# A hybrid decoder layer on one core: the second group's input norm placed beside the first group's attention

## The chip, the cores and the metric

One core of a Trainium2 chip runs the whole layer as one program. The metric is the device time of one execution in microseconds (us), lower being better. Five engines work side by side, each through its own instructions in a fixed order: PE (matrix products and transposes), DVE (elementwise work, reductions, the search for the largest values), ACT (functions and copies), POOL (here it issues the gathers of expert rows) and SP (it issues the other DMA transfers).

## What is computed

1024 tokens of width 1024 pass through one layer: a norm, a projection, retention in 4 heads beside differential attention in 4 heads, an output projection, and then a mixture of 16384 one-neuron experts of which each token uses 128 (8 heads with 16 each).

```
h = rmsnorm(x, norm_mix_g)
rq, rk, rv, rg, dq, dk, dv = split(h @ w_in)
ret_out  = silu(rg) * rmsnorm(retention(rq, rk, rv))
diff_out = rmsnorm(diff_attention(dq, dk, dv, lam), diff_subln_g) * (1 - li)
x = x + concat(ret_out, diff_out) @ w_out
xn = rmsnorm(x, norm_ffn_g)
s = einsum(xn @ peer_wq, subkeys)        # 2 x 128 scores per token and head
pick the 16 largest of each half, then the 16 largest sums: e, g = softmax
x = x + sum over the chosen e of g * gelu(u[e] . xn) * v[e]
out = rmsnorm(x, final_norm_g)
```

## The kernel before

**Groups.** The tokens are cut in tiles of 128. The first group, called sparse, holds tiles 0 to 2, the second, called dense, tiles 3 to 7 (`GROUPS`, line 39). Both pass through the generator `front` (line 140), whose steps are: norm of the input and its transposition (`normed`, line 241, inside `split_t`, line 210); the projections `rv` and `dv` (lines 261 and 262); per head the projections of queries and keys, retention and attention (lines 275 to 404); the gate projection `rg` (line 408); the output projection (lines 423 to 427); a second norm and transposition; and the routing (lines 452 to 492), which in 16 passes projects a query (`psT`, line 458), copies it out of PSUM (`pqT`, line 459), takes scores against 128 keys (`psc`, `sc`, lines 467 and 469) and finds the 16 largest on DVE (lines 473 to 477, and after every second pass 479 to 491). After it the experts of the sparse group are gathered row by row by POOL (lines 891 and 898) and used by DVE, while PE computes all 16384 experts for the dense group (lines 740 to 742 and 818 to 820).

**Numbers in two halves.** A projection writes each operand as a rounded part and a rest and makes three products of it, so every weight chunk of 512 KB is loaded (`wraw`), rounded by ACT (`whi`, line 164) and, in the sparse group, subtracted by DVE (`wlo`, line 166) and stored for the dense group, which loads it again (line 163). Each product of `mm` (line 170) is three matmuls, lines 172 to 174.

**Order.** The generators yield at their seams. `weave(a, b, na, nb)` takes `na` steps of one for `nb` of the other, and `until(g, mark)` runs one to a named seam. Lines 766 to 773 set the order that this change is about:

```
run(until(gs, "mixed"))                                            # sparse attention to its end
run(weave(until(gs, "summed"), until(gd, "normed"), 15, 5))        # output projection | dense input norm
run(weave(until(gd, "projected"), gs, 8, 19))                      # dense rv, dv | sparse routing
```

This is only the order of the program. A planner (`schedule_with_timeline_sim`, line 62) then places the instructions on each engine, in the program's order where nothing speaks against it and otherwise where it expects room, so that later matmuls can stand ahead of earlier ones that have to wait.

**Memory.** PSUM has eight banks: tag `A` twice two banks, `B` twice one, `T` one and `R` one. The sparse group's query projections all use `T` (`proj_t`, line 179). `proj_n` (line 189) takes two tiles at a time in `A`, and the fifth tile of the dense group in `R`. The dense group's input tiles `xt`, its norm weights `gmix` and the scratch `jk` share five rooms of tag `ug` (`big`, line 152). `Routed` (line 494) takes the rooms `sx`, `sa` (sparse) and `la`, `lb` (dense) when it is made.

Of the kernel before, what the change touches and what calls it, by code (L numbers as in the profile page):

```python
# [23 lines left out]
P = 128  # L24
# [75 lines left out]
def layer_kernel(ctx, tc, x, wt, wn, wo, wq, sk, ut, u, v, gmix, gffn, gfin, gsub, dlam, consts, alb, out):  # L100
# [39 lines left out]
    def front(m, pp, cst, g0, nt, dense, late):  # L140
# [11 lines left out]
        def big(shape, name, dt=F32):  # L152
            return m.big[0].tile(shape, dt, tag=m.big[1], bufs=m.big[2], name=name)
# [32 lines left out]
                res.append((a, b, ps))  # L186
            return res

        def proj_n(srcs, xs, done):
            ps = []  # L190
            while len(ps) < nt:
                if nt - len(ps) == 1 and dense:
                    ps.append(pp.tile([P, 512], F32, tag="R", name="psN1"))
                else:
                    two = bankA("psN2")
                    ps += [two[:, 0], two[:, 1]]
            for c, src in enumerate(srcs):
                w = chunk(src, [P, 2, 512])
                for t in range(nt):
                    for k in range(2):  # L200
                        dc = 2 * c + k
                        mm(ps[t], at(xs, slice(None), dc, slice(t * P, (t + 1) * P)), at(w, slice(None), k),
                           dc == 0, dc == DC - 1)
                if c < len(srcs) - 1:
                    yield
            for t in range(nt):
                done(t, ps[t])
            yield
# [17 lines left out]


        def x_in(t):
            xt = big([P, D], "xt")
            SY.dma_start(xt, x[g0 + t])  # L230
            return xt
        if first:
            xts = [x_in(0)]
            gm = m.fp.tile([P, D], F32, tag="R", name="gmix")
        else:
            gm = big([P, D], "gmix")
        SY.dma_start(gm, gmix.to_broadcast([P, D]))
        if first:
            xts += [x_in(t) for t in range(1, nt)]
# [1 line left out]
        def normed(t):  # L241
            ms = m.tp.tile([P, 1], F32, tag="ms", bufs=2, name="ms")
            xt = xts[t] if first else x_in(t)
            jk = m.fp.tile([P, D], BF, tag="yd", name="jk") if first else big([P, D], "jk", BF)
            A.activation(jk, xt, AF.Square, accum_out=ms)
            r = rstd(m.tp, ms, D, "x")
            V.scalar_tensor_tensor(xt, xt, r, gm, op0=ALU.mult, op1=ALU.mult)
            return xt
# [9 lines left out]
            A.activation(dvt, ps, AF.Copy)  # L258
            SY.dma_start(dv_d[g0 + t], dvt)

        yield from proj_n([WN + c for c in range(4)], hx, lambda t, ps: A.activation(rv[:, t], ps, AF.Copy))
        yield from proj_n([WN + 8 + c for c in range(4)], hx, put_dv)
        yield "projected"

        fp, ap = m.fp, m.ap
# [184 lines left out]
        late.nx = nx  # L450

        yield "routing"
        tv = fp.tile([P, nt, PH, 2, K], F32, tag="yd", name="tv")
        ti = fp.tile([P, nt, PH, 2, K], U32, tag="R", name="ti")
        for hp in range(2 * PH):
            h = hp // 2
            qT = wp.tile([P, n], F32, tag="ga", bufs=2, name="pqT")
            for a, b, ps in proj_t(WQ + hp, nx, "TR"):
                A.activation(qT[:, a:b], ps, AF.Copy)
            skt = fp.tile([P, NK], F32, tag="at", bufs=2, name="skt")  # L460
            SY.dma_start(skt, sk[hp])
            sc = fp.tile([P, nt, NK], F32, tag="kT", bufs=2, name="sc")
            for t0 in range(0, nt, 4):
                t1 = min(nt, t0 + 4)
                ps = bankB("psc")
                for t in range(t0, t1):
                    PE.matmul(ps[:, (t - t0) * P:(t - t0 + 1) * P], qT[:, t * P:(t + 1) * P], skt,
                              start=True, stop=True)
                A.activation(sc[:, t0:t1], ps[:, :(t1 - t0) * P].rearrange("p (t k) -> p t k", k=NK), AF.Copy)
            for t in range(nt):  # L470
                a, b = tv[:, t, h, hp % 2], ti[:, t, h, hp % 2]
                s = sc[:, t]
                V.max(a[:, :8], s)
                V.max_index(b[:, :8], a[:, :8], s)
                V.match_replace(s, a[:, :8], s, LOW)
                V.max(a[:, 8:], s)
                V.max_index(b[:, 8:], a[:, 8:], s)
            if hp % 2:
                V.tensor_copy(late.tf[:, :nt, h], ti[:, :, h])
                cd = fp.tile([P, nt, NC2], F32, tag="q20", bufs=2, name="cd")  # L480
                for o, i0, ni, nj in ((0, 0, 2, 16), (32, 2, 2, 8), (48, 4, 4, 4), (64, 8, 8, 2)):
                    V.tensor_tensor(cd[:, :, o:o + ni * nj].rearrange("p t (i j) -> p t i j", j=nj),
                                    tv[:, :, h, 0, i0:i0 + ni, None].to_broadcast([P, nt, ni, nj]),
                                    tv[:, :, h, 1, None, :nj].to_broadcast([P, nt, ni, nj]), op=ALU.add)
                for t in range(nt):
                    c, a, b = cd[:, t], late.cv[:, t, h], late.ci[:, t, h]
                    V.max(a[:, :8], c)
                    V.max_index(b[:, :8], a[:, :8], c)
                    V.match_replace(c, a[:, :8], c, LOW)
                    V.max(a[:, 8:], c)  # L490
                    V.max_index(b[:, 8:], a[:, 8:], c)
            yield

    class Routed:


        def __init__(self, rp, nt, tags):
            n = nt * PH * K
            both = rp.tile([P, 2, n], F32, tag=tags[0], name="late0")
            self.tf = both[:, 0].bitcast(F16).rearrange("p (t h s k) -> p t h s k", t=nt, h=PH, s=2)  # L500
            self.cv = both[:, 1].rearrange("p (t h k) -> p t h k", t=nt, h=PH)
            self.ci = rp.tile([P, nt, PH, K], U32, tag=tags[1], name="late1")
# [183 lines left out]

    gates = []

    def last_dve():
        ins = nc.cur_bb.bb.instructions  # L690
        return next(i for i in reversed(ins) if i.engine == V.engine).name
# [11 lines left out]
    def run(g):  # L703
        for _ in g:
            pass
# [48 lines left out]
    with ExitStack() as es:  # L754
        pf = pool("pf", es, space=bass.MemoryType.PSUM)
        ms, md = SimpleNamespace(), SimpleNamespace()
        with ExitStack() as e2:
# [8 lines left out]
            with ExitStack() as e3:  # L766
                ms.ap = pool("fa", e3)
                run(until(gs, "normed"))
                run(islice(gs, 4))
                front_consts(cst, cp, ms.ap)  # L770
                run(until(gs, "mixed"))
            run(weave(until(gs, "summed"), until(gd, "normed"), 15, 5))
            run(weave(until(gd, "projected"), gs, 8, 19))
        with ExitStack() as e2:
            fd = pool("fd", e2)
            md.tp = md.ap = md.fp = fd
# [92 lines left out]

    def gate(ins):  # L870
        nonlocal nth
        tc.add_manual_dep(ins.ins, gates[min(nth, len(gates) - 1)],
                          mybir.DependencyInfo(mybir.DependencyClass.NoSync, mybir.DependencyReason.DATA),
                          reason="pace of the gathered experts")
        nth += 1

    def row(t, i, name):
# [62 lines left out]
```

## Time and profile before

| | |
|---|---|
| median of 3 runs | 2811.94 us (2809.43 to 2814.86) |
| the profiled execution | 2812.24 us |
| its span | 2810.5 us |
| PE busy | 2681.3 us, 95% |
| DVE busy | 2303.7 us, 82% |
| ACT busy | 997.4 us, 35% |
| POOL busy | 1071.4 us, 38% |

The span is cut by the events of the order above. The sparse group's projections and attention run to about 160 us, its gate projection from 159 to 181, the output projection and the dense input norm to 266, the sparse routing beside the dense `rv` and `dv` to 400, the dense attention to some 800, the dense routing to 980, and the experts from there to the end. Busy shares are averages over all of these, so each question is read from the stretch that it is about.

### The profile page before, as it was taken

The numbers are of one execution on the slowest core, as the hardware profiler recorded it, in microseconds if no ns is written. First come the engines' busy times: TensorE is split into PE (matmuls) and PEld (weight loads), VectorE is DVE, ScalarE is ACT, GpSimd is POOL, SyncE is SP. The second block draws the span as 40 slices with busy tenths as digits, with TensorE's granted clock in tenths as the row PEclk, the third lists the DMA queues.
The fourth block names the chain that finished last, engine by engine and source line by source line (L and its number), as shares of the span: only waits on it lengthen the run. The fifth ranks groups of instructions, "written<-read, shape, count | busy, mean of one in ns | idle before, by whom it ended". The sixth has DMA issues, their size and how long they took to land.

```text
span 2810.5 us, 43147 instructions
## 1 busy us (share of the span) xinstructions
PE 2681.3 (95%) x16043; PEld 2421.6 (86%) x16043; DVE 2303.7 (82%) x4496; ACT 997.4 (35%) x1879; POOL 1071.4 (38%) x782
## 2 busy tenths in 40 slices
PE   7979989888889999999999999999999999999998
PEld 6867888776789999998888888999999999899997
DVE  3554789887478989986999998888998889889987
ACT  4553335554233356772222222222222222223222
POOL 0000004543310000003555556665666567765662
PEclk9989999999989999999999999999999999999999
DMA  7546557877853347799999899898999989989995
GB/s 265 188 177 231 194 191 254 292 276 259 305 193 132 112 150 244 240 281 330 347 347 338 337 374 354 325 348 336 327 344 338 341 333 346 352 317 341 337 348 204
DMA packets 302076, 797.46 MB, mean 284 GB/s; under 512 B 25116, under 2 KB 119336, under 8 KB 297768
## 3 DMA queue, kind: packets, MB, share of 16 engines
q1 hardware_dynamic: 190120, 390.41, 39.2%
q0 software_dynamic: 111744, 404.28, 39.0%
q8 instruction: 126, 2.06, 0.3%
q14 instruction: 86, 0.70, 0.1%
HBM read 698.97 MB, written 95.62 MB: 283 GB/s over the span
## 4 chain that ended last, share of the span: by engine, by line
PE 66%; DVE 8%; DMA 5%; issue 4%; POOL 2%; ACT 1%; SPq 0%; POOLq 0%; DVEq 0%; ACTq 0%
PE psH L742 7%; PE psH L741 7%; PE psH L740 7%; PE psV L818 5%; PE psV L819 5%; PE psV L820 5%; PE kp L820 3%; PE kp L819 3%; PE kp L818 3%; PE psHs L740 3%; PE psHs L742 3%; PE psHs L741 3%; PE psG L613 3%; DVE ug L893 2%; DMA ug<-in_u,idx 2%
## 5 line engine op out<-in xcount | busy, mean ns | idle before, releaser
L891 POOL DMA_INDIRECT ug<-in_u,idx x384 | 529.9, 1380 | 903.5 <-ACT st L615 458.0
L898 POOL DMA_INDIRECT vg<-in_v,idx x384 | 536.1, 1396 | 393.8 <-DVE sa L900 289.8
L893 DVE SCALAR_TENSOR_TENSOR ug<-ug,sx 128x1024 f32<-128x1024 f32 x384 | 458.7, 1223 | 55.5 <-DMA ug<-in_u,idx 54.7
L900 DVE SCALAR_TENSOR_TENSOR sa<-vg,shs,sa 128x1024 f32<-128x1024 f32 x384 | 492.0, 1281 | 10.5 <-DMA vg<-in_v,idx 6.2
L741 PE MATMUL psH<-nl,uh 128*128 128x320 f32 x1424 | 439.5, 309 | 0.0
L740 PE MATMUL psH<-nh,uh 128*128 128x320 f32 x1424 | 439.3, 309 | 0.0
L742 PE MATMUL psH<-nh,ul 128*128 128x320 f32 x1424 | 438.3, 309 | 0.3 <-DVE ul L728 0.3
L818 PE MATMUL psV<-vh,wh 128*128 128x512 f32 x768 | 300.0, 392 | 1.1 <-DVE accl L854 1.1
L819 PE MATMUL psV<-vl,wh 128*128 128x512 f32 x768 | 299.8, 391 | 0.0
L740 PEld LDWEIGHTS psH<-nh,uh 128*128 128x128 f32 x1424 | 267.3, 188 | 5.8
L741 PEld LDWEIGHTS psH<-nl,uh 128*128 128x128 f32 x1424 | 267.3, 188 | 4.8
L742 PEld LDWEIGHTS psH<-nh,ul 128*128 128x128 f32 x1424 | 267.0, 188 | 4.3 <-DVE ul L728 0.6
L726 ACT ACTIVATE uh<-uraw 128x1024 fp32r<-128x1024 f32 x128 | 135.8, 1061 | 321.5 <-PE psH L741 218.0
L743 ACT ACTIVATE ga<-psH 128x320 f32<-128x320 f32 x178 | 75.1, 429 | 447.0 <-PE psH L742 434.2
L740 PE MATMUL psHs<-nh,uh 128*128 128x320 f32 x624 | 195.7, 315 | 6.8 <-ACT ga L743 6.8
L819 PE MATMUL kp<-vl,wh 128*128 128x512 f32 x512 | 200.1, 393 | 0.3 <-DVE vl L842 0.3
L818 PE MATMUL kp<-vh,wh 128*128 128x512 f32 x512 | 194.7, 393 | 4.7 <-ACT wh L834 4.7
L164 ACT ACTIVATE whi<-wraw 128x1024 fp32r<-128x1024 f32 x104 | 109.9, 1058 | 241.2 <-PE psT L173 124.8
L741 PE MATMUL psHs<-nl,uh 128*128 128x320 f32 x624 | 194.1, 311 | 0.0
L742 PE MATMUL psHs<-nh,ul 128*128 128x320 f32 x624 | 192.6, 313 | 0.8 <-DVE ul L728 0.8
L728 DVE TENSOR_TENSOR ul<-uraw,uh 128x1024 fp32r<-128x1024 f32 x128 | 156.9, 1226 | 44.1 <-ACT uh L726 43.9
L820 PE MATMUL psV<-vh,wl 128*128 128x512 f32 x456 | 173.3, 389 | 0.0
(251 smaller groups left out, 6036.4 us busy)
## 6 DMA issues: line engine op xcount, KB each, us to landing
uraw<-in_ut SPq DMA_DIRECT2D x128, 512.0 KB, 6.6
vraw<-in_v SPq DMA_DIRECT2D x128, 512.0 KB, 6.9
g_d<-st SPq DMA_DIRECT2D x80, 512.0 KB, 6.3
gt<-g_d SPq DMA_DIRECT2D x32, 1280.0 KB, 9.6
wl_d<-wlo SPq DMA_DIRECT2D x52, 512.0 KB, 2.9
wlo<-wl_d SPq DMA_DIRECT2D x52, 512.0 KB, 4.3
wraw<-in_wt SPq DMA_DIRECT2D x32, 512.0 KB, 4.4
wraw<-in_wq SPq DMA_DIRECT2D x32, 512.0 KB, 4.6
```

The costliest lines, as they stand in the source:

```text
L726: A.activation(uh, raw, AF.Copy)
L728: V.tensor_sub(ul, raw, uh.bitcast(F32))
L740: PE.matmul(ps, uh[:, dc], xh[:, dc, sl], start=(dc == 0), stop=False)
L741: PE.matmul(ps, uh[:, dc], xl[:, dc, sl], start=False, stop=False)
L742: PE.matmul(ps, ul[:, dc], xh[:, dc, sl], start=False, stop=(dc == DC - 1))
L818: PE.matmul(ps, Wh[e][:, sl], Vh[e][:, so], start=start, stop=False)
L819: PE.matmul(ps, Wh[e][:, sl], Vl[e][:, so], start=False, stop=False)
L820: PE.matmul(ps, Wl[e][:, sl], Vh[e][:, so], start=False, stop=stop)
L891: G.indirect_dma_start(out=ug, out_offset=None, in_=u, in_offset=bass.IndirectOffsetOnAxis(ap=idxA[t][:, k:k + 1], axis=0))
L893: gate(V.scalar_tensor_tensor(ug, ug, 1.0, xt, op0=ALU.mult, op1=ALU.mult, accum_out=hs[:, k:k + 1]))
L898: G.indirect_dma_start(out=vg, out_offset=None, in_=v, in_offset=bass.IndirectOffsetOnAxis(ap=idxA[t][:, k:k + 1], axis=0))
L900: gate(V.scalar_tensor_tensor(ac, vg, hs[:, k:k + 1], ac, op0=ALU.mult, op1=ALU.add))
```

## The change

1. **Order.** The sparse group first goes to its seam "projected" and six steps on; then its attention is woven with the dense input norm, six steps to one. Seven steps of the sparse group follow (four of the gate projection, three of the transposition of its results), then four steps of the dense group (its `rv` projection), then the rest of the output projection. Only `dv` is left to be woven with the sparse routing.
2. **Pace and rooms.** The five dense input tiles use the rooms `sx`, `sa` and `rv` in turn, `gmix` the room `la`, `jk` the room `lb`. Each load of a tile is tied, in the planner's order alone, behind the last DVE instruction that the program held when the load was written. `Routed` takes its rooms when the routing begins.
3. **Banks.** The dense `rv` takes bank `T` and `dv` a bank `B` for the fifth tile in place of `R`. The sparse routing's passes use banks `T` and `R` in turn.

```diff
-        def proj_n(srcs, xs, done):
+        def proj_n(srcs, xs, done, odd="R"):
...
-                    ps.append(pp.tile([P, 512], F32, tag="R", name="psN1"))
+                    ps.append(bankB("psN1") if odd == "B" else pp.tile([P, 512], F32, tag=odd, name="psN1"))
...
         def x_in(t):
-            xt = big([P, D], "xt")
-            SY.dma_start(xt, x[g0 + t])
+            rooms = ((sp, "sx"), (sp, "sa"), (lp, "rv"))[t % 3]
+            xt = rooms[0].tile([P, D], F32, tag=rooms[1], name="xt") if dense else big([P, D], "xt")
+            ins = SY.dma_start(xt, x[g0 + t])
+            if dense:
+                after(ins, last_dve(), "input of the second group")
...
-            gm = big([P, D], "gmix")
+            gm = lp.tile([P, D], F32, tag="la", name="gmix")
...
-            jk = m.fp.tile([P, D], BF, tag="yd", name="jk") if first else big([P, D], "jk", BF)
+            jk = m.fp.tile([P, D], BF, tag="yd", name="jk") if first else lp.tile([P, D], BF, tag="lb", name="jk")
...
-        yield from proj_n([WN + c for c in range(4)], hx, lambda t, ps: A.activation(rv[:, t], ps, AF.Copy))
-        yield from proj_n([WN + 8 + c for c in range(4)], hx, put_dv)
+        yield from proj_n([WN + c for c in range(4)], hx, lambda t, ps: A.activation(rv[:, t], ps, AF.Copy), "T")
+        yield from proj_n([WN + 8 + c for c in range(4)], hx, put_dv, "B")
...
         yield "routing"
+        late.alloc()
...
-            for a, b, ps in proj_t(WQ + hp, nx, "TR"):
+            for a, b, ps in proj_t(WQ + hp, nx, "TR" if dense else "TR"[hp % 2]):
...
-                run(until(gs, "mixed"))
-            run(weave(until(gs, "summed"), until(gd, "normed"), 15, 5))
-            run(weave(until(gd, "projected"), gs, 8, 19))
+                run(until(gs, "projected"))
+                run(islice(gs, 6))
+                run(weave(until(gs, "mixed"), until(gd, "normed"), 6, 1))
+            run(islice(gs, 4 + sn))
+            run(islice(gd, 4))
+            run(until(gs, "summed"))
+            run(weave(until(gd, "projected"), gs, 4, 19))
```

The number of instructions of each kind stays as it was on every engine, but for eight more `ACT_TABLE_LOAD` on ACT. Rows of the built programs show what moved. In them `xt` is a dense input tile, `rg` and `yd` are the sparse group's results of retention and attention, `psX` is a bank of transposes, `ret` and `psS`, `psA`, `pov` are retention's and attention's banks, `hh`/`hl` are the transposed inputs (here the dense group's) and `mh` the transposed results.

**Place 1, PE, between the sparse gate projection and the output projection.** Before, retention's last tile, then:

```order
L293 MATMUL ret<-qT,kT 128x128
L297 MATMUL ret<-pack,kT 128x128
L300 MATMUL ret<-rv,am 128x128
L302 MATMUL ret<-S,qT 128x128
L304 MATMUL ret<-rv,kn 128x128
L220 MATMUL psX<-pack,xt 128x128 x16
L220 MATMUL psX<-pack,rg 128x128 x4
L220 MATMUL psX<-pack,yd 128x128 x4
L172 MATMUL psN_1865<-whi,mh 128x512
```


Now, at the place where the results are transposed:

```order
L173 MATMUL psN_1906<-wlo,hh 128x512
L174 MATMUL psN_1906<-whi,hl 128x512
L220 MATMUL psX<-pack,rg 128x128 x3
L220 MATMUL psX<-pack,yd 128x128
L172 MATMUL psN_1906<-whi,hh 128x512
L220 MATMUL psX<-pack,yd 128x128 x2
```


The sixteen transposes of the dense input are gone from there, and the transposes of the results stand among matmuls of the dense `rv` projection (`psN_1905` to `psN_1907`), of which 75 stand ahead of the first of them.

**Place 2, ACT, in the sparse attention.** Before, from a weight chunk to the next head's exponentials:

```order
L164 ACTIVATE whi<-wraw 128x1024
L278 ACTIVATE qT<-psT 128x384
L377 ACTIVATE e_950,Z<-psS,Z 128x128
L377 ACTIVATE e_952,Z<-psS,Z 128x128
L299 ACTIVATE kn<-ret,c_kdec 128x128
```


Now, from the same chunk of the same head:

```order
L164 ACTIVATE whi<-wraw 128x1024
L281 ACTIVATE qT<-psT 128x384
L248 ACTIVATE jk,ms<-xt 128x1024
L136 ACT_TABLE_LOAD
L136 ACTIVATE rs_x<-ms,eps 128x1
L164 ACTIVATE whi<-wraw 128x1024
L285 ACTIVATE kT<-psT 128x384
L302 ACTIVATE kn<-ret,c_kdec 128x128
L222 ACTIVATE hh<-psX 128x4x128 x2
L164 ACTIVATE whi<-wraw 128x1024
L393 ACTIVATE aT<-psA 128x384
L380 ACT_TABLE_LOAD
L380 ACTIVATE e_996,Z<-psS,Z 128x128
```


A square over an input tile (`jk`), a table load, a root (`rs_x`), two copies out of the transposes' banks (`hh`) and the table load back to the exponentials came in between.

**Place 3, PE, the end of the sparse attention.** Now, after the last key projection of the sparse group and ahead of its gate projection, in part:

```order
L296 MATMUL ret<-qT,kT 128x128
L300 MATMUL ret<-pack,kT 128x128
L303 MATMUL ret<-rv,am 128x128
L305 MATMUL ret<-S,qT 128x128
L307 MATMUL ret<-rv,kn 128x128
L220 MATMUL psX<-pack,xt 128x128 x8
L392 MATMUL psA<-pack,e_1333 128x128
L396 MATMUL pov<-dvh,aT 128x128
L366 LDWEIGHTS ab
L366 MATMUL psS<-ab 128x128
L368 MATMUL psS<-kk,qa_1430 128x128
L369 MATMUL psS<-kk,qb_1432 128x128
```


In 76 such rows, with 16 of the 40 transposes of the dense input, no projection matmul stands; before, 47 rows lay between the last key projection and the gate projection, none of them of the dense group.

**Place 4, PE, the sparse routing** (with buffer numbers: a pass's `psT_2388` is copied to `pqT_2380`, eight lower, and `psT_2502` to `pqT_2494`). Before:

```order
L172 MATMUL psT_2388<-nh_2166,whi_2383 128x384
L173 MATMUL psT_2388<-nl_2167,whi_2383 128x384
L174 MATMUL psT_2388<-nh_2166,wlo_2384 128x384
L467 MATMUL psc_2417<-skt_2414,pqT_2380 128x128 x3
L172 MATMUL psT_2466<-nh_2166,whi_2461 128x384
```


Now:

```order
L172 MATMUL psT_2580<-nh_2314,whi_2575 128x384
L173 MATMUL psT_2580<-nl_2315,whi_2575 128x384
L174 MATMUL psT_2580<-nh_2314,wlo_2576 128x384
L172 MATMUL psT_2637<-nh_2314,whi_2632 128x384
L173 MATMUL psT_2637<-nl_2315,whi_2632 128x384
L471 MATMUL psc_2531<-skt_2528,pqT_2494 128x128 x3
L174 MATMUL psT_2637<-nh_2314,wlo_2633 128x384
```


Before, the score matmuls `psc` of a pass follow directly on its own query projection. Now 26 matmuls of the next two passes stand between them, in the other bank.

## Rows read from the trace of the kernel before

**Rows 1.** Stretches: us, busy time and count by engine, PE clock, DMA share, GB/s.

```profile
80.00:181.70 101.70, 94.97 (x576) 84.67 (x575) 51.97 (x113) 62.18 (x177) 0.00 (x0) 1.00 0.52 179
181.70:266.00 84.30, 67.97 (x319) 54.91 (x320) 46.25 (x87) 38.65 (x78) 0.00 (x0) 0.86 0.67 236
266.00:400.00 134.00, 122.86 (x676) 112.10 (x674) 97.88 (x599) 42.29 (x64) 0.00 (x0) 1.00 0.56 193
...
2000.00:2780.00 780.00, 780.00 (x4385) 711.72 (x4384) 690.25 (x793) 200.34 (x286) 495.51 (x349) 1.00 0.91 335
...
180.00:200.00 20.00, 6.58 (x29) 4.62 (x29) 11.96 (x35) 12.33 (x32) 0.00 (x0) 0.61 0.73 260
```

**Rows 2.** Waits of PE, 150:215 (first row) and 280:400: total, times, longest.

```profile
PE psX L220 <- DVE xt L247: 9.4, 2, 7.9
...
PE psc L467 <- ACT pqT L459: 6.3, 5, 1.3
PE psN L172 <- ACT whi L164: 4.8, 5, 1.0
```

**Rows 3.** Timeline of PE: start us, duration us; neighbours in two stretches.

```profile
207.67 0.63 PE L172 MATMUL psN<-whi,mh 128*128 128x512 f32 x1
208.09 0.43 PE L173 MATMUL psN<-wlo,mh 128*128 128x512 f32 x1
...
262.28 1.25 PE L220 MATMUL psX<-pack,xn 128*128 128x128 f32 x8 [0.74 <-DVE nl L223]
263.29 0.94 PE L172 MATMUL psN<-whi,hh 128*128 128x512 f32 x3
...
264.54 0.39 PE L172 MATMUL psN<-whi,hh 128*128 128x512 f32 x1
264.77 0.39 PE L173 MATMUL psN<-wlo,hh 128*128 128x512 f32 x1
```

**Rows 4.** PE by line in 181.7:266: count, busy us, mean ns, idle before.

```profile
L174 PE MATMUL psN<-whi,ml 128*128 128x512 f32 x48 | 19.3, 403 | 0.0
...
L172 PE MATMUL psN<-whi,hh 128*128 128x512 f32 x26 | 9.9, 393 | 0.0
...
L220 PE MATMUL psX<-pack,xt 128*128 128x128 f32 x40 | 7.6, 335 | 9.8 <-DVE xt L247 9.4 <-ACT yd L396 0.4
```

**Rows 5.** PE by line in 266:400.

```profile
L174 PE MATMUL psN<-whi,hl 128*128 128x512 f32 x58 | 22.7, 392 | 0.0
```

**Rows 6.** Timeline of ACT around a table load in the gap.

```profile
186.21 0.35 ACT L299 ACTIVATE kn<-ret,c_kdec 128x128 f32<-128x128 f32 x1
186.57 1.28 ACT L136 ACT_TABLE_LOAD   x1
187.87 0.29 ACT L136 ACTIVATE rs_x<-ms,eps 128x1 f32<-128x1 f32 x1
```

**Rows 7.** ACT by line in 160:220.

```profile
L245 ACT ACTIVATE jk<-xt 128x1024 bf16<-128x1024 f32 x5 | 5.3, 1062 | 2.3 <-DMA xt<-in_x 2.3
L222 ACT ACTIVATE hh<-psX 128x512 fp32r<-128x512 f32 x7 | 4.1, 598 | 1.4 <-PE psX L220 1.4
```

**Rows 8.** Timeline: last key projection, an attention tile's start and end, first gate projection.

```profile
149.98 0.42 PE L174 MATMUL psT<-hh,wlo 128*128 128x384 f32 x1
...
153.01 0.33 PE L365 MATMUL psS<-kk,qa 128*128 128x128 f32 x1 [0.28 <-DVE kk L340]
...
159.30 0.50 PE L172 MATMUL psN<-whi,hh 128*128 128x512 f32 x1
...
160.56 0.36 ACT L395 ACTIVATE jk<-pov,rz 128x128 bf16<-128x128 f32 x1
```

**Rows 9.** Timeline: DVE's first selection of the routing; ACT's first step after the last one.

```profile
276.90 0.68 DVE L473 MAX8 tv<-sc 128x8 f32<-128x128 f32 x3
...
405.65 1.28 ACT L546 ACT_TABLE_LOAD   x1
```

More of the change, by code (lines that the diff above doesn't have):

```diff
@@ L494, in layer_kernel, with __init__, alloc @@
     class Routed:
-        def __init__(self, rp, nt, tags):
+        def __init__(self, *room):
+            self.room = room
+        def alloc(self):
+            rp, nt, tags = self.room
             n = nt * PH * K
@@ L687, in layer_kernel, with after @@
     gates = []
+    def after(ins, other, reason):
+        tc.add_manual_dep(ins.ins, other, mybir.DependencyInfo(mybir.DependencyClass.NoSync,
+                                                               mybir.DependencyReason.DATA), reason=reason)
     def last_dve():
@@ L871, in gate @@
         nonlocal nth
-        tc.add_manual_dep(ins.ins, gates[min(nth, len(gates) - 1)],
-                          mybir.DependencyInfo(mybir.DependencyClass.NoSync, mybir.DependencyReason.DATA),
-                          reason="pace of the gathered experts")
+        after(ins, gates[min(nth, len(gates) - 1)], "pace of the gathered experts")
         nth += 1
```

## The prediction

> **What bounds the kernel now.** I first asked the stretches which engine is full where. From 2000 to 2780 us PE is busy for 780 of 780 us, and the reader is to see that nothing else there is [rows 1]: a microsecond saved ahead of the experts is one saved at the end, provided that what feeds them moves along. So the question is how much time PE loses ahead of them, in the places that the diff touches. Two stand out. From 181.7 to 266 it is busy for 68.0 of 84.3 us, and the granted clock over it is 0.86; in 180 to 200 alone it works 6.6 of 20 us at 0.61 [rows 1]. From 266 to 400 it works 122.9 of 134 [rows 1].
>
> Then the waits name the cause. In the first place PE waits 9.4 us in two pieces for the multiplied input tile of the dense group [rows 2]: all 16 transposes of that tile and the next stand ahead of the transposes of the sparse results (place 1), and nothing is left to do beside them. The timeline shows what such a pause costs afterwards: two 512-column matmuls start 0.42 us apart at 207.67 and 0.23 us apart at 264.54 [rows 3]. PE ran at the lower of its two levels, 1.2 GHz, after the pause, and at 2.4 GHz later. In the second place it waits 6.3 us in five pieces for the copied query and 4.8 us in five for a rounded chunk [rows 2].
>
> **The gap, priced.** I count what PE had to do in 181.7 to 266 at the full clock. There are 3 x 48 matmuls of the output projection and about 3 x 26 of the dense projection [rows 4], together 222 at 0.23 us [rows 3], 51 us. There are 40 transposes of the dense input [rows 4] and 48 others of the same shape; eight took from 262.28 to the next matmul at 263.29 [rows 3], 0.13 us each, so 11.4 us. Retention's last tiles add some 2 us. That makes 64.4 of 84.3 us, so 20 us were lost. In the new order 75 matmuls of the dense `rv` projection, 17 us, stand between the gate projection and the first transpose of its results, and its remaining 45 stand among these. They have no open condition but a weight chunk each, so they cover the silu, the roots and the 24 multiplications. I take back 19 of the 20 us and leave 1 for a chunk that is late. The bounds are 20 and, if half of the cover is late, 10.
>
> **The norm beside attention, priced.** ACT gets five squares of 1.06 us, ten copies of 0.60 us [rows 7] and eight more table loads of 1.28 us [rows 6], together 21.5 us, and five short roots. From 80 to 181.7 it is busy for 62.2 of 101.7 us, DVE for 52.0 [rows 1], so there is room for this on both. Three of the five steps lie beside query and key projections of 24 matmuls each; I cost them at nothing, since ACT had 39.5 us free there. If that cover is gone, a step delays the copy that frees bank `T` by up to its own 4.8 us (1.06 + 2 x 0.60 + 2 x 1.28).
>
> Two steps fall into place 3, where no projection stands. Before, that stretch went from 149.98 to 159.30, 9.3 us [rows 8]. Now two squares, two table loads and four copies come into ACT's order there, 2.1 + 2.6 + 2.4 = 7.1 us, and one attention tile that used to lie beside projections. I take 18 us, of which 16 transposes at 0.13, 2 us, are work that is no longer in the gap. So 7 us are newly lost. The bounds are 0 and 20 (all of ACT's 21.5 us late). The gate projection cannot start earlier: its two pairs of banks `A` are those of the scores.
>
> A rule speaks against this part. The row shows a load of 1.28 us that starts 0.01 us after the end of its predecessor and is followed after 0.02 us [rows 6]. The Trainium skill, "ScalarE: Activation LUTs", section "What ACT_TABLE_LOAD costs", gives 1283 ns for the load and about 1380 ns more for a drain, 2.66 us for every switch. By that page the two loads of the stretch cost 2.8 us more and the forecast below would be 2797; the trace has no such drain, so I stay with the row.
>
> **The routing, priced.** It kept PE for 134 us, of which 6.3 + 4.8 = 11.1 were waits [rows 1, 2]. It held 3 x 58 matmuls of the dense projections [rows 5]; now it holds 60, so 114 at 0.23 us, 26 us, have gone into the gap, where they are the cover. What stays for PE is 122.9 - 26 = 97 us. DVE was busy for 97.9 us of it [rows 1] and keeps all of that. So after the change the two are level, and the routing can take hardly less than 98 us and a start. The alternating banks remove the wait for the copy: a pass's scores now stand 26 matmuls behind its projection (place 4), 26 x 0.17 = 4.4 us by the spacing of the shorter matmuls that I estimate from 0.23 x 384 / 512, where 0.47 us of copying are to be hidden. I take 5 us of loss in place of 11.1, so 6 us back. The bounds are all 11 back, and the worst of the rivals below.
>
> What has no price. Five input loads of 512 KB move on SP among the weight chunks of the attention. Each waits for a room whose last reader is three tiles back, and what queues behind it, the next chunk and a chunk's store, has four buffers; the DMA engines are at 0.52 there and at 0.67 in the gap [rows 1]. If that cover is gone, the price is the 2.3 us for which ACT waited on such loads [rows 7]. `dv` holds one bank `B` into the routing, so the transposes of the second norm and `psc` share the other; matmuls of `dv` stand between them. If they did not, six banks would each cost about a copy, 6 x 0.60 = 3.6 us. POOL's order in front of its first gathers does not change. The later rooms of `Routed` cost no instruction.
>
> **The sum.** -19 + 7 - 6 = -18 us. The profiled execution took 2812.24 us, 1.7 more than its span and 0.3 above the median of the three runs, so this gives **2794 us**. DVE gives a second look at it: from its first selection at 276.90 to ACT's step after the last at 405.65 are 129 us [rows 9], and with at most 98 busy no more than 31 can come out. The 18 lie inside. The attention that follows is laid out anew by the planner, in rows that differ by single places; I give that 6 us either way. So the likeliest case spans 2784 to 2804. About 0.2%, 5.6 us, is what a measurement of this kernel can tell from no change.
>
> **Rivals.**
> - *The end of the attention is serial.* From its first score matmul at 153.01 to the square of its result at 160.56 a tile takes 7.6 us [rows 8]. If the four tiles of place 3 go nearly one after the other instead of two abreast, the stretch takes 30 to 35 us instead of 18, and PE has there what the gap had: short work between pauses, after which it fell to 0.61 [rows 1]. The loss is 20 to 25 instead of 7, and the result 2807 to 2812. For it: table loads sit ahead of exponentials. Against: two banks `A` let two tiles overlap, and did so before.
> - *A pass of the routing is bound by its chain.* This one ends slower. The 16 passes took 128.75 / 16 = 8.0 us each [rows 9], while DVE worked 6.1 and PE after the change needs 6.1. If projection, copy, scores, copy, selection and the rest of the next chunk follow one another so that a pass stays at 8.0 us, the dense matmuls that left leave 26 us of holes: -19 + 7 + 26 = +14, 2826 us. It decides from 7.9 us a pass on (126 us in all, 0.2% slower). Against: place 4, which puts two projections ahead of the scores.
> - *The change does not do what it says.* The pace binds only the planner. But the rows have the five steps apart, and the gap's transposes are gone. If the hole only moves, 2812.
> - *More than forecast.* With all 20 and all 11 us back and the stretch hidden: 2781.
>
> **How the numbers follow.** The forecast 0.62, the serial end 0.18 (0.06 of it faster by over 0.2%, 0.12 within), the chain-bound pass 0.10, no effect 0.03, more than forecast 0.07. Faster 0.62 + 0.06 + 0.07 = 0.75, within 0.2% 0.15, slower 0.10. From 2781 to 2811 all is taken in but the chain-bound pass, part of the serial end and half of the best case, together about 0.18.
>
> **What would show it.** Right: PE's wait for the dense input tile is gone, the clock near the output projection is 1.00, the routing starts near 266 as before, but with all of `rv` done, its selections take 100 to 108 us from the first to the last, the wait of `psc` for the copied query is gone, and the experts start 12 to 24 us earlier. Wrong: a stretch ahead of the gate projection of over 30 us with a lower clock, selections that still take 125 us, or a later attention of the dense group that gives the time back.

## The result and the profile after

The changed kernel took **2845.11 us** (median of 4 runs, 2840.16 to 2848.0) beside 2812.1 us for the kernel before: a ratio of 1.0109, with a 95% interval of 1.0092 to 1.0127. The forecast was 2794 us, its range 2781 to 2811, and faster than before.

The experts are as full as before [rows 1], so the loss lies ahead of them. The landmarks below are starts of single instructions in the PE timelines (in DVE's for the two selections and POOL's for the gather); the end is the span of the profiled execution, 2810.5 us before and 2845.8 after.

| us | before | after | difference |
|---|---|---|---|
| last sparse key projection | 149.98 | 164.25 | +14.3 |
| first sparse gate projection | 159.30 | 196.40 | +37.1 |
| first query projection of the sparse routing | 267.71 | 307.35 | +39.6 |
| its last | 393.85 | 403.42 | +9.6 |
| first, last sparse selection | 276.90, 403.03 | 321.06, 419.18 | +44.2, +16.2 |
| first gathered row | 439.31 | 458.77 | +19.5 |
| first dense gate projection | 665.13 | 677.91 | +12.8 |
| its last | 698.03 | 728.43 | +30.4 |
| end of the span | 2810.5 | 2845.8 | +35.3 |

So 37 us are lost beside the sparse attention, some 28 come back up to the end of the routing, and 18 more are lost in the dense gate projection, far from any line of the diff. The same stretches in windows (the columns are those of [rows 1]; the window of the dense gate projection runs on 3 us behind its last start), of the kernel before first:

```profile
80.00:149.98 69.98, 66.76 (x426) 62.53 (x426) 38.15 (x80) 43.30 (x127) 0.00 (x0) 1.00 0.55 190
149.98:159.30 9.32, 7.45 (x55) 5.83 (x53) 6.77 (x17) 6.72 (x23) 0.00 (x0) 1.00 0.51 178
159.30:267.71 108.41, 90.45 (x424) 72.63 (x424) 53.29 (x102) 50.81 (x106) 0.00 (x0) 0.89 0.61 213
267.71:393.85 126.14, 116.36 (x638) 106.49 (x636) 94.19 (x574) 40.37 (x61) 0.00 (x0) 1.00 0.55 193
665.10:701.00 35.90, 33.07 (x164) 27.32 (x163) 25.10 (x68) 14.79 (x29) 13.15 (x13) 0.99 0.86 309
```

And of the changed kernel:

```profile
80.00:164.25 84.25, 71.29 (x410) 66.05 (x409) 41.13 (x80) 53.34 (x127) 0.00 (x0) 0.92 0.48 171
164.25:196.40 32.15, 18.54 (x105) 15.00 (x105) 18.15 (x40) 21.09 (x60) 0.00 (x0) 0.73 0.27 91
196.40:307.35 110.95, 105.19 (x481) 84.56 (x479) 39.12 (x78) 43.62 (x83) 0.00 (x0) 0.97 0.60 209
307.35:403.42 96.07, 93.28 (x534) 89.54 (x534) 84.92 (x506) 32.34 (x52) 0.00 (x0) 0.98 0.63 219
677.90:731.40 53.50, 41.14 (x181) 33.33 (x181) 29.73 (x77) 17.82 (x39) 18.08 (x16) 0.84 0.68 238
2000.00:2780.00 780.00, 780.00 (x4386) 711.90 (x4385) 690.79 (x793) 200.45 (x286) 506.71 (x351) 1.00 0.91 338
```

The reader is to see two good rows and three bad ones. From the gate projection to the routing PE idles 5.8 us in place of 18.0, and its clock is 0.97 in place of 0.89. In the routing it idles 2.8 us in place of 9.8. But up to the last key projection PE idles 13.0 us in place of 3.2 and its clock is 0.92 in place of 1.00. Place 3 went from 9.3 to 32.2 us, with PE at work for 18.5 of them at a clock of 0.73, and the dense gate stage went from 35.9 to 53.5 us with PE idle for 12.4.

**Place 3** reads as one chain. SP's timeline, 165 to 194 us of the changed kernel:

```profile
165.51 0.37 SPq L353 DMA_DIRECT2D dvh<-dv_d  x1
165.93 0.48 SPq L231 DMA_DIRECT2D xt<-in_x  x1
...
167.64 1.30 SPq L231 DMA_DIRECT2D xt<-in_x  x1
170.62 0.91 SPq L346 DMA_DIRECT2D kd_d<-kk  x2
193.51 0.37 SPq L353 DMA_DIRECT2D dvh<-dv_d  x1
```

SP's waits, 120 to 200:

```profile
SPq L167 <- DVE wlo L166: 36.1, 5, 12.2
SPq L353 <- PE pov L396: 26.6, 2, 21.9
```

The same stretch on ACT:

```profile
175.04 1.06 ACT L248 ACTIVATE jk<-xt 128x1024 bf16<-128x1024 f32 x1 [2.03 <-DMA xt<-in_x]
...
176.20 1.28 ACT L136 ACT_TABLE_LOAD   x1
177.50 0.29 ACT L136 ACTIVATE rs_x<-ms,eps 128x1 f32<-128x1 f32 x1
...
180.58 0.60 ACT L222 ACTIVATE hh<-psX 128x512 fp32r<-128x512 f32 x1 [1.42 <-PE psX L220]
181.43 0.60 ACT L222 ACTIVATE hh<-psX 128x512 fp32r<-128x512 f32 x1 [0.26 <-PE psX L220]
182.47 0.28 ACT L393 ACTIVATE aT<-psA 128x128 f32<-128x128 f32 x1 [0.44 <-PE psA L392]
182.76 1.28 ACT L380 ACT_TABLE_LOAD   x1
```

And PE's waits, 140 to 200:

```profile
PE psX L220 <- DVE rs_x L137: 4.7, 1, 4.7
PE ret L296 <- ACT rv L315: 3.4, 1, 3.4
PE psS L366 <- ACT e L380: 3.4, 2, 1.8
PE psT L172 <- ACT qT L281: 2.0, 1, 2.0
```

The last input tiles are issued at 165.93 and 167.64, behind a load of `dvh` that had itself waited. ACT stands at the square until the tile is there. Root, product and transposes follow one by one, and attention's exponentials stand behind all of it, after a second table load. No wait is over 5 us. Of the 23 us that place 3 grew by, 11.7 are more idle time of PE, some 5 are the clock (an estimate: 18.5 us at 0.73), and the rest is more work, the 16 transposes among it. How much of this the late tiles themselves cost is asked below.

**The dense gate stage** is another mechanism. POOL gathers a row of experts into one of five rooms (`UG`), and DVE's product with it frees the room. DVE's order at the place, with a row's place in the gathering as its buffer number (24402 is row 82, and three more is the next). Before:

```
754 L893 SCALAR_TENSOR_TENSOR ug_24408,shs_24155<-ug_24408,sx_24151 128x1024
759 L295 TENSOR_TENSOR am_5867<-ret_5865,c_intra_290 128x128
761 L306 SCALAR_TENSOR_TENSOR S_86<-S_86,ret_5865 128x128
762 L893 SCALAR_TENSOR_TENSOR ug_24402,shs_24155<-ug_24402,sx_24151 128x1024
763 L893 SCALAR_TENSOR_TENSOR ug_24405,shs_24155<-ug_24405,sx_24151 128x1024
```

Now rows 87, 88 and 89 stand ahead of row 82, which 83, 85 and 86 follow, with retention's `am` between them and its `S` behind:

```
804 L907 SCALAR_TENSOR_TENSOR ug_24417,shs_24155<-ug_24417,sx_24151 128x1024
805 L298 TENSOR_TENSOR am_5865<-ret_5863,c_intra_286 128x128
806 L907 SCALAR_TENSOR_TENSOR ug_24420,shs_24155<-ug_24420,sx_24151 128x1024
807 L907 SCALAR_TENSOR_TENSOR ug_24423,shs_24155<-ug_24423,sx_24151 128x1024
808 L309 SCALAR_TENSOR_TENSOR S_86<-S_86,ret_5863 128x128
809 L907 SCALAR_TENSOR_TENSOR ug_24402,shs_24155<-ug_24402,sx_24151 128x1024
```

DVE's timeline there, and under it POOL's (start, duration, and in brackets the idle time before):

```profile
686.21 1.22 DVE L907 SCALAR_TENSOR_TENSOR ug<-ug,sx 128x1024 f32<-128x1024 f32 x1 [3.84 <-DMA ug<-in_u,idx]
687.36 0.28 DVE L298 TENSOR_TENSOR am<-ret,c_intra 128x128 f32<-128x128 f32 x1
692.03 1.23 DVE L907 SCALAR_TENSOR_TENSOR ug<-ug,sx 128x1024 f32<-128x1024 f32 x1 [4.38 <-DMA ug<-in_u,idx]
697.75 1.23 DVE L907 SCALAR_TENSOR_TENSOR ug<-ug,sx 128x1024 f32<-128x1024 f32 x1 [4.49 <-DMA ug<-in_u,idx]
698.90 0.28 DVE L309 SCALAR_TENSOR_TENSOR S<-S,ret 128x128 f32<-128x128 f32 x1
```

```profile
687.71 0.94 POOL L905 DMA_INDIRECT ug<-in_u,idx  x1 [6.55 <-DVE am L298]
693.53 0.94 POOL L905 DMA_INDIRECT ug<-in_u,idx  x1 [4.88 <-DVE ug L907]
699.26 1.88 POOL L905 DMA_INDIRECT ug<-in_u,idx  x1 [4.79 <-DVE S L309]
```

Rows 82, 83, 85 and 86 have come and hold four rooms, as their products stand behind. One room is left, so row 88 is gathered after the product of row 87 and row 89 after that of 88. From product to product that takes 5.8 us; DVE waits 3.8, 4.4 and 4.5 us for the three rows, 12.7 in all, and retention, which needs `S`, waits with it. (POOL's releaser in brackets is the instruction of DVE next to the product.) PE then waits for retention's copy, and later for the rest `wlo` of a weight chunk, which SP loads behind a load of the routing's keys that had waited for retention's matmul. PE's waits in the stage, 677.9 to 731.4, and SP's, 677 to 735:

```profile
PE ret L296 <- ACT rv L315: 5.1, 1, 5.1
PE psN L173 <- DMA wlo<-wl_d: 3.5, 1, 3.5
```

```profile
SPq L465 <- PE ret L303: 14.4, 2, 9.5
```

### The profile page after: what moved, and what is told of

Its sections match the earlier page's. It is cut to its first block, busy times and chain, and to the rows that moved or that the text cites. A ratio compares the mean times of both kernels' runs of the same rounds, so it can differ in the third digit from the quotient of the medians.

```text
span 2845.8 us, 43164 instructions
## 1 busy us (share of the span) xinstructions
PE 2699.9 (95%) x16043; PEld 2441.1 (86%) x16043; DVE 2304.2 (81%) x4496; ACT 1006.3 (35%) x1887; POOL 1083.0 (38%) x782
## 4 chain that ended last, share of the span: by engine, by line
PE 76%; DVE 11%; DMA 5%; issue 4%; ACT 2%; POOL 1%; SPq 0%; DVEq 0%; POOLq 0%; ACTq 0%
PE psH L754 7%; PE psH L753 7%; PE psH L752 7%; PE psV L834 6%; PE psV L835 6%; PE psV L836 6%; PE kp L836 4%; PE kp L835 4%; PE kp L834 4%; PE psHs L752 3%; PE psHs L754 3%; PE psHs L753 3%; PE psG L621 3%; PE psT L172 2%; PE psT L173 2%
## 5 line engine op out<-in xcount | busy, mean ns | idle before, releaser
L912 POOL DMA_INDIRECT vg<-in_v,idx x384 | 542.4, 1413 | 389.0 <-DVE sa L914 280.8
```

Source lines behind the costliest of these rows:

```text
L912: G.indirect_dma_start(out=vg, out_offset=None, in_=v, in_offset=bass.IndirectOffsetOnAxis(ap=idxA[t][:, k:k + 1], axis=0))
```

## The experiments

**The banks alone** (kernel before, fifth tiles of `rv` and `dv` in a bank `B`; the edit in part):

```diff
-            for a, b, ps in proj_t(WQ + hp, nx, "TR"):
+            for a, b, ps in proj_t(WQ + hp, nx, "TR" if dense else "TR"[hp % 2]):
```

> The kernel before with the banks of the change alone (routing in T and R in turn, the fifth tile of both dense projections in B). By the forecast's third term the waits of the routing (11.1 us) fall to 5: 2806 us, bounds 2801 to 2812. Rival: with all 120 third products of the dense projections still inside the routing, PE is full there anyway and the banks give nothing by themselves: 2812.

Measured: 2808.5 us, ratio 0.9974 (0.9962 to 0.9985), 7 us faster. The third term holds in the time. By landmarks the routing takes 12.4 us less (113.7 in place of 126.1), while the stretch from the gate projection to it grows by 7.4, which was not traced.

**The place of the norm.** One edit each to the changed kernel (the remark behind a line names the run):

```diff
-                run(weave(until(gs, "mixed"), until(gd, "normed"), 6, 1))
+                run(weave(until(gs, "mixed"), until(gd, "normed"), 3, 1))          # three to one
...
-                run(until(gs, "projected"))
-                run(islice(gs, 6))
-                run(weave(until(gs, "mixed"), until(gd, "normed"), 6, 1))
+                run(weave(until(gs, "projected"), until(gd, "normed")))             # early
+                run(until(gs, "mixed"))
...
-                after(ins, last_dve(), "input of the second group")                 # no pace
```

> The changed kernel with the weave of attention and dense norm at 3:1 in place of 6:1, so that all five norm steps stand beside projections and none in the stretch behind the last key projection. Theory A (the loss sits in that stretch, where nothing is left to run beside the norm): the stretch from the last key projection to the first gate projection falls from 32 us to 10 to 15, and the time to 2815 to 2825 us. Theory B (each norm step beside attention delays an in-order engine, wherever it stands): the loss is spread over the heads and the time stays at 2838 to 2850.

> The changed kernel with the dense norm woven one to one with the sparse group's own rv and dv projections, ahead of all attention; everything behind it as in the change. Theories A and B both say that the 28 us lost in the attention go: gate projection starts near 161 to 170 us in place of 196, and, if the later loss in the dense gate projection is a consequence of the sparse group's being late, the time is 2785 to 2800. If that later loss (18 us) has nothing to do with it: 2805 to 2818. Rival (the loss comes from rv in front of the output projection or from the banks): still 2840.

> The changed kernel without the tie of the input loads to a vector instruction: three of the five loads then stand on the load queue ahead of the sparse projections, two stay where rooms come free. Theory C (the loads come late on the queue, behind stores and loads that wait, and the square behind them stops ACT): the first three steps cost nothing and the time falls by 10 to 20, to 2825 to 2835. Theory B: 2840 to 2850, as what the steps cost is ACT's and the banks' order, not the load.

| | time | ratio | last key projection | first gate projection | dense gate stage, first to last |
|---|---|---|---|---|---|
| the change | 2845.1 | 1.0109 (1.0092 to 1.0127) | 164.3 | 196.4 | 677.9 to 728.4 |
| 3:1 | 2812.1 | 0.9996 (0.9986 to 1.0006) | 166.4 | 178.9 | 660.9 to 694.3 |
| early | 2816.1 | 1.0003 (0.9990 to 1.0016) | 152.6 | 161.9 | 648.4 to 701.8 |
| no pace | 2819.1 | 1.0017 (1.0006 to 1.0028) | 160.5 | 171.3 | 651.3 to 703.1 |

At 3:1 place 3 shrinks to 12.5 us, as theory A said, but the attention ahead of it is as late as in the change, as theory B said: five steps beside projections cost 16.5 us, three cost 14.3. Without the pace 25 of the 37 us come back, more than theory C gave; but the planner also placed the steps anew, so this alone is no proof of it. With the norm early nearly all 37 come back, and the routing ends 20.4 us ahead of the kernel before. Yet the time stays, since the dense gate stage takes 53 us, where the change's takes 51 by the same count. At 3:1 it takes 33. That 3:1 should differ points away from lateness and to the order on DVE: the change, the early and the no-pace kernel have rows 87 to 89 ahead of 82, the kernel before, the banks and 3:1 have not.

**Products in the order of the gathers.** A tie for the planner, beside the loop's own (in part):

```diff
+        if last is not None:
+            after(ins, last, "products in the order of the gathers")
+        last = ins.ins.name
         after(ins, gates[min(nth, len(gates) - 1)], "pace of the gathered experts")
```

> The changed kernel with one tie more: each product with a gathered row stands behind the product of the row gathered before it. In the change, the products of rows 87, 88 and 89 stand on DVE ahead of those of rows 82 and 83 and of retention's last steps. Theory D (the 18 us that the dense gate projection lost are the three latencies of these rows): the stretch from its first to its last matmul falls from 50 us to 32 to 35, and the time to 2825 to 2830. Rival (the rows are late because the sparse group is 16 us late, in whatever order they are used): 2840 to 2850.

> The same tie in the kernel with the dense norm beside the sparse rv and dv projections, which reached its routing's end 20 us ahead of the kernel before and lost as much in the dense gate projection. Theory D: 2790 to 2798. Rival: 2812 to 2818 as without the tie.

> The kernel before with the same tie. Its products of rows 84 and 81 stand ahead of 82 and 79 too, but one at a time. Theory D says that only the three in a row cost: 2808 to 2814. If being out of sequence costs by itself, everywhere: 2795 to 2805.

Measured: the change with it 2824.5 us, ratio 1.0041 (1.0023 to 1.0059); the early norm with it **2796.6 us, 0.9955 (0.9938 to 0.9971)**, faster than both kernels; the kernel before with it 2809.3, 0.9995 (0.9980 to 1.0009). The stage in the change with the tie (first row) and in the early kernel with it (second):

```profile
674.90:715.40 40.50, 35.00 (x163) 28.82 (x162) 26.87 (x71) 15.38 (x29) 15.21 (x14) 0.92 0.79 287
```

```profile
643.90:678.90 35.00, 32.55 (x164) 27.04 (x163) 27.05 (x71) 15.47 (x29) 15.63 (x14) 1.00 0.89 333
```

Theory D is borne out: the change gains 0.7% by the tie and the early norm 0.5%, and to the kernel before, which had no three in a row at this place, the tie gives nothing. From first to last matmul the stage falls from 53.4 to 32.0 us with the early norm. In the change it falls from 50.5 to 37.5, not to the 32 to 35 that was expected: PE still waits 3.8 us there for the rest of one chunk, and its clock is 0.92. Ahead of the dense attention the change's program is the same with the tie as without; behind it the planner placed other instructions anew too, so the whole gain in time cannot be laid to the three products, but the loss in this stage can.

**What the 36 us beside the attention are.** All with the tie. Without the root (a reciprocal of the mean square on DVE); with the loads on POOL; with both and 3:1; and, beyond these three, with only loads, transposes and copies left of the norm. The edits in part:

```diff
-            r = rstd(m.tp, ms, D, "x")
+            V.tensor_scalar(r, ms, 1.0 / D, EPS, op0=ALU.mult, op1=ALU.add)      # dense group alone
+            V.reciprocal(r, r)
...
-            ins = SY.dma_start(xt, x[g0 + t])
+            ins = (G if dense else SY).dma_start(xt, x[g0 + t])
...
             xt = xts[t] if first else x_in(t)
+            if dense:
+                return xt
```

> The changed kernel with the tie and without the square roots of the dense input norm (the norm divides by the mean square instead of its root), so that ACT has eight table loads fewer. Theory E (the table loads in ACT's order delay the attention): the first gate projection starts 10 us earlier than with the roots by the trace's 1.28 us a load, 20 us earlier if each load drains for as long again, and the time falls by as much. Theory C (input loads that come late on the queue and what waits behind them): it starts within 4 us of the run with the roots.

> The change with the tie, and the five input loads of the dense norm issued by POOL, which has nothing else to do there, in place of SP; the norm's steps stand on PE and ACT where they stood. Theory C (the squares wait for loads that SP issues late, behind stores and loads that wait themselves): the first gate projection starts at 178 to 186 us in place of 197, and the time falls to 2806 to 2814. Theory B (what the steps cost is ACT's and the banks' order): 193 to 198 us, 2820 to 2826.

> The change with the tie and with all three cures of the runs before at once: the weave at 3:1, the input loads on POOL, and no square root in the dense input norm (left out, so no table loads). One by one they moved the first gate projection by -17.5, -8.2 and -10.8 us. If these are three separate parts of the 36 us that the norm cost beside the attention, it starts at 161 to 165 us, as with the norm ahead of the attention, and the time is 2788 to 2800. If they are one delay seen three times (the same late chain), it starts no earlier than 172 us and the time is 2802 to 2810.

> The kernel with the three cures, and of the dense input norm only loads, transposes and the copies out of their banks: squares, scales and the products with the norm's weights are left out. Theory F (the rest of the loss is the transposes and their banks, and the copies in ACT's order): the first gate projection still starts at 177 to 182 us. Theory G (it is the chain of load, square, scale and product in front of each transpose): it starts at 162 to 170 us.

| | last key projection | first gate projection | place 3 between them | ratio |
|---|---|---|---|---|
| change, in sequence | 165.3 | 197.5 | 32.2 | 1.0041 (1.0023 to 1.0059) |
| no root | 158.5 | 186.7 | 28.2 | 1.0003 (0.9992 to 1.0015) |
| loads on POOL | 158.1 | 189.3 | 31.2 | 1.0012 (0.9997 to 1.0027) |
| all three cures | 161.8 | 181.1 | 19.3 | 0.9986 (0.9973 to 1.0000) |
| transposes alone | 157.2 | 173.7 | 16.5 | 0.9948 (0.9937 to 0.9960) |
| early norm | 152.5 | 161.8 | 9.3 | 0.9955 (0.9938 to 0.9971) |

Each cure helps by itself: the loads by 8.2 us, the table loads by 10.8, the place by 17.5 (in the kernels without the tie). The loads stand between theory C and theory B, and 7.2 of their 8.2 us are gained ahead of the last key projection: with the tiles there in time ACT no longer waits for one in place 3, and place 3 still takes 31.2 us at a clock of 0.73. So the late tiles are not what makes place 3 long. With no step of the norm in it, it takes 12.5 us at 3:1 and 19.3 with all three cures; there the planner also leaves more of the attention for it, 86 PE instructions against 66. The sum of the three is 36.5, as much as the early norm gives (35.7); but the three together give 16.5, no more than 3:1 by itself. So they are not three parts, and that expectation fell; the other one, one delay seen three times, fits the numbers.

The last run stands between its two theories: 7 of the 19 us that are left are the norm's squares, scales and products, 12 are what loads, transposes, copies and subtractions cost by standing among the attention. The early norm has the same 40 transposes ahead of its gate projection, so the 12 are not their own work. From 40 us on, with the transposes alone (first row) and with the early norm (second):

```profile
40.00:173.69 133.69, 121.29 (x713) 109.82 (x711) 65.26 (x124) 70.93 (x184) 1.58 (x3) 0.96 0.58 201
```

```profile
40.00:161.79 121.79, 114.28 (x706) 104.76 (x704) 72.08 (x134) 78.48 (x199) 0.00 (x0) 1.00 0.64 220
```

PE idles 12.4 us in place of 7.5, and its clock is worth another 5 (an estimate: 121.3 us at 0.96). Whether the idle time comes from ACT's order or from the two banks `B`, which the transposes share with attention's `psA` and `pov`, no run tells apart.

**The other two terms, with the early norm and the tie.** The dense `rv` projection back beside the routing, its fifth tile in a bank `B`; the routing back in one bank; and the loads without the pace (edit above). The first two, in part:

```diff
-            run(islice(gd, 4))
...
-            run(weave(until(gd, "projected"), gs, 4, 19))
+            run(weave(until(gd, "projected"), gs, 8, 19))                         # no cover
...
-            for a, b, ps in proj_t(WQ + hp, nx, "TR" if dense else "TR"[hp % 2]):
+            for a, b, ps in proj_t(WQ + hp, nx, "TR"):                            # one bank
```

> The early norm with the tie, but the dense rv projection back beside the sparse routing (its fifth tile in a bank B, as T is the routing's there). It prices the cover of the first term alone: if the 75 and 45 matmuls are what covers the silu, the roots and the transposes, PE stands idle there for 8 to 12 us and the time is 2802 to 2812, against 2796 with them. Rival: the routing absorbs it, as DVE is no longer the bound with dense matmuls beside it: within 3 us of 2796.

> The early norm with the tie, and the sparse routing in the one bank T as before the change. It prices the third term by itself: with 60 in place of 120 third products of dense projections beside it, the routing has less to hide its waits with, so by the forecast's 11.1 - 5 = 6 us the time is 2802, bounds 2796 to 2812. Rival: the cover that left was hiding them, and the passes become bound by the chain of projection, copy, scores and copy, 20 us or more: 2815 or later.

> The early norm with products in sequence, without the tie of the input loads to a vector instruction. If the late loads are a cost of the tie, wherever the norm stands, the first gate projection starts 2 us earlier (159 to 160 us) and the time is 2790 to 2796. If they are a cost of the place (beside stores and loads that wait), it changes nothing: 2794 to 2800; and if loads that come too early take the DMA engines from the first weights, it is slower: 2800 or more.

Without the cover: 2798.3 us, 0.9950 (0.9934 to 0.9966), the same as with it, as the rival said. The first row is its gap, the second its routing, in which PE is full; the third is the gap with the cover:

```profile
161.70:266.60 104.90, 88.38 (x391) 68.92 (x390) 40.52 (x81) 39.42 (x81) 0.00 (x0) 0.92 0.55 191
266.60:379.75 113.15, 112.28 (x623) 104.96 (x624) 87.17 (x523) 38.60 (x60) 0.00 (x0) 1.00 0.60 214
```

```profile
161.80:279.56 117.76, 107.06 (x482) 85.28 (x481) 40.48 (x82) 44.92 (x89) 0.00 (x0) 0.97 0.55 197
```

Its routing ends 6.5 us later than with the cover (379.75 against 373.27), and at the start of the dense gate projection 0.9 are left of it (644.79 against 643.87). So `rv` covers something, but nothing of it that can be measured reaches the end.

In one bank: 2805.2 us, 0.9976 (0.9962 to 0.9989). The routing ends 18.8 us later; by the two ratios some 6 of these reach the end. Its stretch, and the wait that comes back (PE, 279 to 392):

```profile
279.00:392.00 113.00, 96.64 (x539) 89.29 (x540) 94.03 (x575) 34.18 (x53) 0.00 (x0) 0.98 0.53 188
```

```profile
PE psc L471 <- ACT pqT L463: 14.4, 11, 1.3
```

That is nearly the rival's 20 us at the routing's end and the term's 6 in the time. Without the pace: 2801.3 us, 0.9958 (0.9941 to 0.9974), the same as with it, with a gate projection 4 us later (165.75). So with the early norm the tie costs nothing; in the change, leaving it out had given 25 us back. It took the tie and that place together.

## Why the prediction was wrong

**The gap (-19) was right in size, and only partly for its reason.** Time that PE idled, and time lost to the clock (its busy time times what the clock lacks, an estimate from the windows), were 18.0 + 9.9 = 27.9 us from the gate projection to the routing before, and 5.8 + 3.2 = 9.0 after: 19 back. Not all of it is the cover's: the early norm without the cover loses 16.5 + 7.1 = 23.6 us there, and with it 10.7 + 3.2 = 13.9. So some 4 us come from the norm's leaving, 10 from the cover, and for the other 5 no run stands alone. What I missed is how little of this reaches the end. Without the cover the same matmuls lie in the routing, PE is full there (0.9 us idle), and the whole cover is worth 6.5 us at the routing's end and nothing that can be measured in the time. What in the dense attention takes these 6.5 back was not traced.

**The norm beside the attention (+7) was the step that failed.** It cost 37.1 us up to the gate projection, against the 18 - 9.3 = 8.7 on which the term rested. "I cost them at nothing, since ACT had 39.5 us free there" failed first: three steps beside projections cost 14.3 us. ACT was free in sum, but each step is a chain through SP, ACT, DVE, PE and ACT again, in queues that keep their order, and attention's own steps stand behind it. My bound of 4.8 us a step, for the case that the cover is gone, gives 14.4 for three, but that it meets the 14.3 is luck: 9.7 of these are idle time of PE, the clock at 0.92 is worth over 5 more (an estimate, from 71.3 us of work), and five steps cost 16.5, not 24. Then the stretch of 18 us took 32.2. The rival of the serial end said 30 to 35 with a lower clock, and of this stretch it was right; its 2807 to 2812 lacked the 14.3 ahead of it and what the dense attention lost.

**The five input loads "among the weight chunks" were no detail.** I priced them at 2.3 us from the waits of before. Moved to another queue they gave 8.2, as on SP they stand behind transfers that wait themselves: from 120 to 200 us the stores of `wlo` waited 36.1 us for DVE, the loads of `dvh` 26.6 for their rooms. Most of the 8.2 lie ahead of place 3.

**The table loads** cost about what the row said. Eight of them, with the five roots, were left out for 10.8 us, 1.35 for each load, beside 1.28 in [rows 6]; as the cures do not add up, this is no measure of a single load. By the Trainium skill, "ScalarE: Activation LUTs", section "What ACT_TABLE_LOAD costs", with a drain of about 1380 ns more, they would be 21, an estimate; no run here shows that.

**The routing (-6) was right.** Its idle time went from 9.8 to 2.8 us, the wait of `psc` is gone, the selections take 98 us, and the banks alone gave 7. The rival of the chain-bound pass did not come; the run in one bank shows that it would have, in part, without the alternation. Its line of 7.9 us a pass does not follow from its own sum: +14 at 8.0 falls to +5.6, the 0.2%, at 7.5.

**"I give that 6 us either way" was the second step that failed.** The attention that is laid out anew lost 18 us at one place, 13 of them by the order of the rows on DVE, as the tie shows. The program's order shows these rows; the prediction read it only at the places of the diff.

Together: +37.1 beside the attention, +2.5 to the routing's start (with the `rv` matmuls in it), -30.0 in the routing without them, +9.6 at its end, and +35.3 at the end of the span, 17.6 of it in the dense gate projection.

## What to carry to other kernels

Free time of an engine in sum is no cover: price a moved step by the longest chain through queues that keep their order, and at least once by the full delay that it can hand on. Work that waits on little is the better neighbour: the same norm, beside projections with no attention among them, cost 2.5 us in place of 37. And where a planner lays out a rotating set of rooms, tie the uses to the order of the fills, or a small shift elsewhere can leave one room in rotation.

## What was not expected of the hardware

With one room free a gathered row takes 4.3 us from its issue at 687.71 to its product at 692.03, and 5.8 from product to product. That is then the whole rate, while the DMA engines are at 0.68 of their time in that stage. And the granted clock falls in a stretch without one wait of 5 us: 0.73 from 164.25 to 196.40, where PE was busy for 18.5 of 32.2 us.
